# Attention scores per head on 64 rows of the array with plain keys, and the adaLN sums of layer 1 beside the dense SwiGLU

## The chip, the core and the metric

The kernel runs on one core of a Trainium2 chip. The metric is the device time of one execution in microseconds, from the first to the last instruction and what lies around them; the tensors start and end in the chip's main memory.

## The reference, cut to what matters

Two decoder layers over 256 tokens of width 1024, in fp32. Each layer takes six modulation vectors (shift, scale and gate, for the mixer and for the feed-forward part) from one product of a 1024-vector with a 1024 x 6144 matrix. Layer 0 ends in a dense SwiGLU, layer 1 in a mixture of eight experts.

```python
c_act = jax.nn.silu(c)
for l in range(DEPTH):                                    # 2 layers
    mod = (c_act @ w_ada[l] + b_ada[l])[:, None, :]
    sh_a, sc_a, g_a, sh_f, sc_f, g_f = jnp.split(mod, 6, axis=-1)
    h = rmsnorm(x, norm_mix[l]) * (1.0 + sc_a) + sh_a
    x = x + g_a * hybrid_mixer(h, ...)
    h = rmsnorm(x, norm_ffn[l]) * (1.0 + sc_f) + sh_f
    f = swiglu(h, ...) if l % 2 == 0 else moe_swiglu(h, ...)
    x = x + g_f * f

# one of the four mixers (4 heads of 64); the others differ in mask, bias or weighting
sco = jnp.einsum('bqhd,bshd->bhqs', qb, k) * scale
p = masked_softmax(sco, s_idx[None, :] <= t[:, None])
o = jnp.einsum('bhqs,bshd->bqhd', p, v)
```

Per layer five score products of this kind are made: stick-breaking (`c`), dilated (`b`), forgetting (`d`), and the selected and window branches of sparse attention (`s`, `w`, whose keys and values all heads share).

## The kernel before, in words

Features lie on partitions, 8 tiles of 128 x 256 tokens. A weight comes in 1 MB pieces into a buffer (`raw`), and ScalarE and VectorE split each half of it into a rounded fp32r part and its remainder (tiles `w`); every projection is then three fp32r matmuls of 256 columns (`mm3`: high x high, high x low, low x high). A ring of four such half pieces lets the split run up to three halves ahead of TensorE. The expert stage works on raw fp32 weights instead.

The program is a row of such chunks: 12 input chunks (`pcq`, `pck`, `pt`), 16 merge gates (`mg`) with four branch projections (`br`) between them, four output chunks (`wo`), then for layer 0 eleven rounds of `w1`, `w3` and `w2` (tiles `fa`, `fg`, `f`), then layer 1 in the same way, then the experts. Beside it run generators ("threads"): one for each attention unit, and `ada_thread` for the modulation vectors that are not needed at once. `Weave` puts their steps between the chunks: it keeps a clock of its own for each engine (`Clock`, with a cost for each instruction) and takes a step when its inputs are ready by that clock. This settles each engine's order of instructions when the program is built; on the chip every engine goes through its own list in order. At some places a chunk cannot go on without a thread, and `until` then takes the thread's steps at once, ready or not: before each branch projection, and before the last `wo` and the last `w2` chunk, where all threads must have ended.

One modulation vector is one sum of `ada_thread`: four 1 MB loads into the one buffer `aux` (the next load starts when VectorE has read the last one), eight VectorE instructions that add a row of 1024 weights times a scalar into `adaacc`, then four matmuls with ones (`ada`), a copy, two transposes (`adat`) and an addition (`mod`). `ADA_MIX` and `ADA_FFN` list the sums (layer, vector) for the two mixers and for the dense SwiGLU, and `STEP_MIX` and `STEP_FFN` the least distance of two loads by the clock of `Weave`. `GAPS` lists vectors made in another way, on TensorE, at the norms (`adag`).

Scores: `transp_k` writes the keys of two heads into a zero-padded block (`kT`, 128 rows x 2 x 256), so that one matmul over all 128 rows yields both heads' scores side by side: queries 0 to 127 against 128 keys (bank `s0`), queries 128 to 255 against 256 keys (banks `s1a`, `s1b`). `softmax` or `stick` makes the weights, `pT` transposes them (`tc`, `tb`, `td`, `ts`, `tw`), and `pv` multiplies them with the values: two heads stand on the two column halves of the array (64 columns each), in matmuls of 128 columns (`oc`, `ob`, `od`, `oa`). All of these are plain fp32, where one matmul is two instructions of TensorE.

Of the kernel before, what the change touches and what calls it, by code (L numbers as in the profile page):

```python
# [21 lines left out]
F32 = mybir.dt.float32  # L22
# [28 lines left out]

ADA_MIX = (((0, 2), (0, 4), (0, 3)), ((1, 4), (1, 3)))
ADA_FFN = ((1, 1), (1, 0))
STEP_MIX = (14.0, 18.0)
STEP_FFN = 15.0
GAPS = ((0, 5), (1, 2), (1, 5))
# [232 lines left out]
class Clock:  # L289
# [216 lines left out]
def trunk(ctx, tc, A):  # L506
# [462 lines left out]
    def mixer(l, mb, mp, pre):  # L969
# [83 lines left out]

        def key_blocks(t, ps):

            for j in range(2):
                r = slice(j * DH, (j + 1) * DH)
                sc.activation(t[r, :, j, :], ps[r, :].rearrange("p (a k) -> p a k", a=2), AF.Copy)
# [23 lines left out]


        def scores(name, q, k, kshared=None):
            tk = [None]
            yield lambda: rx.take(3, tk, name)
            s0 = px(name + "s0")
            s1 = [px(name + "s1a"), px(name + "s1b")]
            for p in range(2):
                kt = k[:, p if kshared is None else kshared]  # L1090
                pe.matmul(s0[:, p * S:(p + 1) * S], q[:, p, 0:P], kt[:, :, 0:P], start=True, stop=True)
            yield
            for p in range(2):
                kt = k[:, p if kshared is None else kshared]
                pe.matmul(s1[p], q[:, p, P:S], kt, start=True, stop=True)
                yield
            cm["S" + name] = (s0, s1, tk)

        def softmax(name, m0, m1, gate=None, out=None):
# [23 lines left out]
            for a in range(2):  # L1123
                pp = p1[:, 2 * a:2 * a + 2, :]
# [4 lines left out]
                dv.tensor_reduce(mx[:, 4 + 2 * a:6 + 2 * a], pp, axis=AX.X, op=OP.max, negate=True)  # L1129
                yield  # L1130
                exps(1, p1, (2 * a, 2 * a + 1))
                yield
# [12 lines left out]
        def stick(name):  # L1145
# [12 lines left out]
            gp.memset(u1[:, :, S:S + 1], 1.0)  # L1158
            sc.activation(t0, s0.rearrange("p (h k) -> p h k", h=NH), AF.Tanh, scale=0.0625)
            yield  # L1160
            for a in range(2):
                sc.activation(t1[:, 2 * a:2 * a + 2, :], s1[a].rearrange("p (h k) -> p h k", h=2), AF.Tanh, scale=0.0625)
                yield
# [43 lines left out]
        def pv(mi, name, parts, extra=None):  # L1207

            ko_ = [None]
            yield lambda: rO.take(1, ko_, name)  # L1210
            yield "sync"
            ps = pt("o" + name)
            n_mm = 0
            for p in range(2):
                for i in range(2):
                    for j in range(2):
                        h = 2 * p + j
                        out = ps[j * DH:(j + 1) * DH, p * S + i * P:p * S + (i + 1) * P]
                        ops = []
                        for (t0, t1, _), v in parts:  # L1220
                            ops.append((v(0, h), t0[:, h, i * P:(i + 1) * P]))
                            if i:
                                ops.append((v(1, h), t1[:, h, :]))
                        if extra is not None:
                            ops.append(extra(h, i))
                        for n, (lh, rh) in enumerate(ops):
                            pe.matmul(out, lh, rh, start=(n == 0), stop=(n == len(ops) - 1), tile_position=(0, j * DH))
                        n_mm += len(ops)
# [119 lines left out]

        def cmp_extra(h, i):
            return (cm["vc"][:, h, :], cm["pcT"][:, i * P:(i + 1) * P])  # L1350

# [37 lines left out]

        def caus0():  # L1390
            return C("C")[:, None, :].to_broadcast([P, NH, P])

# [17 lines left out]
        def unit_b():  # L1410
# [10 lines left out]
            rq1.give(tk)  # L1421
            yield from softmax("b", C("ln0")[:, None, :].to_broadcast([P, NH, P]),
                               lambda a: C("ln1")[:, None, :].to_broadcast([P, 2, S]))
# [4 lines left out]
        def unit_d():  # L1428
# [12 lines left out]
            FB, kp = cm["FB"]  # L1441
            yield from softmax("d", FB[:, :, 0:P], lambda a: FB[:, 2 * a:2 * a + 2, P:384], out=(FB, kp))
            yield from pT("d")
# [11 lines left out]
        def unit_a():  # L1455
# [12 lines left out]
            yield from scores("s", TP["ar"], TP["kk"], 0)  # L1468
            yield from softmax("s", caus0(), caus1, g3[:, :, :, 1])
# [4 lines left out]
            yield from softmax("w", caus0(), caus1, g3[:, :, :, 2])  # L1474
            yield from pT("w")
# [36 lines left out]
        else:  # L1512
            ps = pm("pck")
            feat_chunk(("in", l, 1), ps)
        key_blocks(ckT, ps)
        mark("ck")
# [676 lines left out]
```

## Time and profile before

| | before |
|---|---|
| timed, median of 3 | 1500.13 us (1496.19 to 1501.11) |
| profiled execution, own time | 1492.01 us |
| its span, first to last instruction | 1490.2 us |
| TensorE matmul busy | 1428.5 us (96%) |
| VectorE busy | 654.9 us (44%) |
| ScalarE busy | 501.9 us (34%) |
| DMA | 446.67 MB, mean 300 GB/s |

A busy share is an average over stages: start (to 37 us of the span), mixer of layer 0 (to about 291), dense SwiGLU (to about 491), mixer of layer 1 (to about 756), experts (to the end). TensorE is busy nearly all the time in the first four, while the DMA engines are nearly full only among the experts.

### The profile page before, as it was taken

The page shows a single profiled execution, that of the slowest core. Times are in us where ns is not written, and L with a number is a line of the kernel's source. Part 1 is how long each engine was busy: PE and PEld are TensorE (multiplying, and loading weights), DVE is VectorE, ACT ScalarE, POOL GpSimd, SP SyncE. Part 2 cuts the span into 40 slices and gives each one's busy share as a digit, 9 for nine tenths or more (in the row PEclk, how much of TensorE's full clock was granted, in tenths as well). Part 3 has the DMA queues.
Part 4 walks back from the last instruction along what each step waited for, and adds up shares of the span by engine and source line. Part 5 has one row for each costly group of instructions (what it writes and reads, how often), then busy time and mean ns, then how long its engine had stood idle before and what let it go on. Part 6 is the DMA issues. An engine that isn't in the chain of part 4 may idle for free. (4 is left out here: it accounts for less than half of the span.)

```text
span 1490.2 us, 28386 instructions
## 1 busy us (share of the span) xinstructions
PE 1428.5 (96%) x12156; PEld 1078.0 (72%) x12156; DVE 654.9 (44%) x1167; ACT 501.9 (34%) x996; POOL 56.2 (4%) x58
## 2 busy tenths in 40 slices
PE   7999999999999999999989999989999999999996
PEld 6998998899999899998975555445555555555553
DVE  5797787666665698677641111111111111111111
ACT  3645553354444554655431121111111111111110
POOL 0000011200000100011200000000000000000000
PEclk9999999999999999999999999999999999999998
DMA  9574747787671465554987999999999998989940
GB/s 385 217 264 145 251 173 268 310 305 274 234 247 61 174 222 218 172 197 142 356 333 318 419 419 419 419 419 420 420 416 379 414 420 348 394 344 420 420 200 33
DMA packets 73778, 446.67 MB, mean 300 GB/s; under 512 B 8080, under 2 KB 8464, under 8 KB 29072
## 3 DMA queue, kind: packets, MB, share of 16 engines
q1 hardware_dynamic: 72896, 443.76, 76.1%
q8 instruction: 122, 2.00, 0.5%
q10 hardware_dynamic: 720, 0.59, 0.1%
q14 instruction: 40, 0.33, 0.1%
HBM read 443.27 MB, written 1.05 MB: 298 GB/s over the span
## 5 line engine op out<-in xcount | busy, mean ns | idle before, releaser
L393 PE MATMUL uv<-raw,x 128*64 128x256 f32 x2816 | 340.3, 383 | 8.7 <-DMA raw<-in_moe_w 4.5
L393 DVE TENSOR_TENSOR w<-raw,w 128x1024 fp32r<-128x1024 f32 (+1 forms) x210 | 258.0, 1242 | 105.9 <-ACT w L393 105.5
L393 PEld LDWEIGHTS uv<-raw,x 128*64 128x64 f32 x2816 | 200.9, 137 | 136.8 <-issue 48.6
L393 ACT ACTIVATE w<-raw 128x1024 fp32r<-128x1024 f32 (+1 forms) x210 | 217.4, 1047 | 105.8 <-PE fa L393 16.6
L393 DVE TENSOR_TENSOR es<-es,uv 128x128 f32<-128x128 f32 x88 | 25.4, 288 | 436.2 <-ACT es L393 436.2
L393 PE MATMUL mg<-hh,w 128*128 128x256 f32 x1024 | 188.9, 283 | 4.9 <-DVE w L393 4.2
L393 PE MATMUL y<-raw,at 128*64 128x512 f32 x704 | 169.8, 601 | 11.8 <-PEq L1952 8.1
L393 PEld LDWEIGHTS mg<-hh,w 128*128 128x128 f32 x1024 | 158.6, 189 | 7.9 <-DVE w L393 5.0
L393 PE MATMUL mg<-hl,w 128*128 128x256 f32 x512 | 142.9, 279 | 0.0
L393 ACT ACTIVATE at<-at 128x128 f32<-128x128 f32 x88 | 24.4, 278 | 301.0 <-PE at L393 301.0
L393 PE MATMUL pt<-w,hh 128*128 128x256 f32 (+1 forms) x640 | 113.7, 280 | 0.0
L393 PEld LDWEIGHTS y<-raw,at 128*64 128x64 f32 x704 | 47.4, 136 | 81.1 <-issue 70.8
L393 PEld LDWEIGHTS pt<-w,hh 128*128 128x128 f32 x640 | 97.7, 188 | 1.4 <-issue 1.4
L393 PEld LDWEIGHTS mg<-hl,w 128*128 128x128 f32 x512 | 96.6, 189 | 1.0 <-issue 1.0
L393 PE MATMUL pt<-w,hl 128*128 128x256 f32 (+1 forms) x320 | 89.2, 279 | 0.0
L393 ACT ACTIVATE es<-uv 128x128 f32<-128x128 f32 x88 | 24.4, 278 | 139.6 <-PE uv L393 139.6
L393 PE MATMUL uvo<-raw,x 128*32 128x256 f32 x1056 | 65.9, 380 | 0.0
L393 PE MATMUL fa<-hh,w 128*128 128x256 f32 x352 | 65.7, 285 | 0.0
L393 PE MATMUL fg<-hh,w 128*128 128x256 f32 x352 | 64.0, 281 | 0.0
L393 PE MATMUL f<-fah,w 128*128 128x256 f32 x352 | 63.9, 281 | 0.0
L393 DVE SCALAR_TENSOR_TENSOR adaacc<-aux,cact,adaacc 128x1024 f32<-128x1024 f32 x49 | 63.5, 1297 | 0.0
L393 PEld LDWEIGHTS pt<-w,hl 128*128 128x128 f32 x320 | 60.2, 188 | 0.0
(403 smaller groups left out, 2060.3 us busy)
## 6 DMA issues: line engine op xcount, KB each, us to landing
raw<-in_moe_w SPq DMA_DIRECT2D x263, 1024.0 KB, 16.7
raw<-in_w_in SPq DMA_DIRECT2D x54, 1024.0 KB, 5.0
aux<-in_w_ada SPq DMA_DIRECT2D x48, 1024.0 KB, 7.2
raw<-in_ffn_w SPq DMA_DIRECT2D x33, 1024.0 KB, 5.2
raw<-in_w_branch SPq DMA_DIRECT2D x8, 1024.0 KB, 5.1
raw<-in_w_out SPq DMA_DIRECT2D x8, 1024.0 KB, 5.1
raw<-in_w_in_tail SPq DMA_DIRECT2D x2, 576.0 KB, 3.8
xT<-in_x SPq DMA_DIRECT2D x1, 1024.0 KB, 5.3
```

The lines of the kernel that those rows point to most:

```text
L393: r = f(*args, **kw)
```

## The change: what it does

**Scores.** Keys are kept plain (two heads on the two halves of the partitions, no zeros). Each head has a matmul of its own over 64 rows, at row 0 or row 64 of the array; heads alternate between the halves, and the two halves write to different banks (`s0a`, `s0b`; `s1a`, `s1b`, which now hold heads 0, 2 and 1, 3). `s0b` is a bank of another pool. `softmax` and `stick` read the first block in two instructions in place of one.

**Values.** `pv` takes both query blocks in one matmul where it can (256 or 512 columns) and alternates the two column halves at every matmul.

**Sums.** Layer 1's vectors 4 and 3 move from the second mixer to the dense SwiGLU, whose `ada_thread` has four sums in place of two; its step goes from 15 to 9.5. The second mixer has none. The cost of a matmul in `Clock` now counts the share of rows as well.

```diff
-ADA_MIX = (((0, 2), (0, 4), (0, 3)), ((1, 4), (1, 3)))
-ADA_FFN = ((1, 1), (1, 0))
+ADA_MIX = (((0, 2), (0, 4), (0, 3)), ())
+ADA_FFN = ((1, 1), (1, 0), (1, 4), (1, 3))
 STEP_MIX = (14.0, 18.0)
-STEP_FFN = 15.0
+STEP_FFN = 9.5
...
-            return 2.4e-3 + c * (out.partition_size() / P if tiled else 1.0)
+            return 2.4e-3 + c * (out.partition_size() * ins[0].partition_size() / (P * P) if tiled else 1.0)
...
-        kT = {n: mp.tile([P, 2, 2, S], F32, name=n) for n in ("kT0", "kT1")}
-        for t in kT.values():
-            gp.memset(t, 0.0)
-        ckT = kT["kT0"]
+        ckT = mp.tile([P, 2, S], F32, name="ckT", tag="kT0")
...
-            t = kT[tag]
-            key_blocks(t, ps)
+            t = mp.tile([P, 2, S], F32, name=name, tag=tag)
+            sc.activation(t, ps.rearrange("p (a k) -> p a k", a=2), AF.Copy)
...
-            s0 = px(name + "s0")
+            s0 = [px(name + "s0a"), pa(name + "s0b")]
             s1 = [px(name + "s1a"), px(name + "s1b")]
-            for p in range(2):
-                kt = k[:, p if kshared is None else kshared]
-                pe.matmul(s0[:, p * S:(p + 1) * S], q[:, p, 0:P], kt[:, :, 0:P], start=True, stop=True)
...
+            def prod(out, h, q0, n):
+                p, j = divmod(h, 2)
+                r = slice(j * DH, (j + 1) * DH)
+                pe.matmul(out, q[r, p, q0:q0 + P], k[r, p if kshared is None else kshared, 0:n], start=True, stop=True,
+                          tile_position=(j * DH, 0))
...
+            for h in range(NH):
+                prod(s0[h % 2][:, h // 2 * P:(h // 2 + 1) * P], h, 0, P)
+            yield
+            for h in range(NH):
+                prod(s1[h % 2][:, h // 2 * S:(h // 2 + 1) * S], h, P, S)
...
-            dv.scalar_tensor_tensor(p0, s0.rearrange("p (h k) -> p h k", h=NH), 0.125, m0, op0=OP.mult, op1=OP.add)
+            for a in range(2):
+                dv.scalar_tensor_tensor(p0[:, a::2, :], s0[a][:, 0:S].rearrange("p (h k) -> p h k", h=2), 0.125, m0(a),
+                                        op0=OP.mult, op1=OP.add)
...
+            def run(ops):
+
+                for n in range(len(ops[0])):
+                    for j in range(2):
+                        cols, q0, lh, rh = ops[j][n]
+                        out = ps[j * DH:(j + 1) * DH, :].rearrange("p (a q) -> p a q", a=2)[:, cols, q0:]
+                        pe.matmul(out, lh, rh, start=(n == 0), stop=(n == len(ops[0]) - 1), tile_position=(0, j * DH))
```

The built programs show where the instructions went. First TensorE, at the stick-breaking scores of the second mixer, between two input chunks (`pt`). Before:

```order
L393 MATMUL pt_5703<-w_5606,hl 128x256
L393 MATMUL cs_5733<-kT_5566,cqT 128x256 x2
L393 MATMUL cs1a<-kT_5566,cqT 128x512
L393 MATMUL cs1b<-kT_5566,cqT 128x512
L393 MATMUL pt_5703<-w_5635,hh 128x256 x2
```

Of the changed kernel, at the same place:

```order
L393 MATMUL pt_5746<-w_5653,hl 128x256
L393 MATMUL cs0a<-ckT,cqT 128x128
L393 MATMUL cs0b<-ckT,cqT 128x128
L393 MATMUL cs0a<-ckT,cqT 128x128
L393 MATMUL cs0b<-ckT,cqT 128x128
L393 MATMUL cs1a<-ckT,cqT 128x256
L393 MATMUL cs1b<-ckT,cqT 128x256
L393 MATMUL cs1a<-ckT,cqT 128x256
L393 MATMUL cs1b<-ckT,cqT 128x256
L393 MATMUL pt_5746<-w_5682,hh 128x256 x2
```

The place is the same; four matmuls with 1536 columns in all became eight with 1536 columns in all, each on half of the rows.

Second VectorE, at the end of the dense SwiGLU: `fact` and `fal` are the last round's product and its remainder, the two `w` behind them the second half of the last `w2` piece and the first half of the next layer's first input piece, `xT` the residual after the last `w2` chunk. Before:

```order
L393 TENSOR_TENSOR fal_5326<-fact_5324,fah_5325 128x512
L393 TENSOR_TENSOR w_5330<-raw_4910,w_5330 128x1024
L393 TENSOR_TENSOR w_5359<-raw_4973,w_5359 128x1024
L393 SCALAR_TENSOR_TENSOR xT<-f_3422,mod_3589,xT 128x256 x2
L393 SCALAR_TENSOR_TENSOR xT<-f_3423,mod_3589,xT 128x256 x2
```

Of the changed kernel (`aux_5237`, `aux_5389` and so on are loads that follow each other in the one buffer `aux`):

```order
L393 TENSOR_TENSOR w_5331<-raw_4904,w_5331 128x1024
L393 SCALAR_TENSOR_TENSOR adaacc_5206<-aux_5237,cact,adaacc_5206 128x1024
L393 TENSOR_TENSOR w_5361<-raw_4967,w_5361 128x1024
L393 SCALAR_TENSOR_TENSOR adaacc_5206<-aux_5237,cact,adaacc_5206 128x1024
L393 SCALAR_TENSOR_TENSOR adaacc_5206<-aux_5389,cact,adaacc_5206 128x1024 x2
L393 SCALAR_TENSOR_TENSOR adaacc_5206<-aux_5393,cact,adaacc_5206 128x1024 x2
L393 COPY adaacc_5206<-ada_5399 128x256
L393 TENSOR_TENSOR mod_5408<-adat_5405,bada 128x8
L393 TENSOR_SCALAR adaacc_5410<-aux_5397,cact 128x1024
L393 SCALAR_TENSOR_TENSOR adaacc_5410<-aux_5397,cact,adaacc_5410 128x1024
L393 SCALAR_TENSOR_TENSOR adaacc_5410<-aux_5413,cact,adaacc_5410 128x1024 x2
L393 SCALAR_TENSOR_TENSOR adaacc_5410<-aux_5417,cact,adaacc_5410 128x1024 x2
```

Two more instructions (on `aux_5421`), a copy and a `mod` follow, and only then `xT`. So the second half of the third sum and the whole fourth sum stand in one piece ahead of the residual, and they read six loads (`aux_5389` to `aux_5421`) one after the other.

Third TensorE at the same end of the SwiGLU, of the changed kernel (before, `f` chunk follows `f` chunk with nothing between):

```order
L393 MATMUL f_3419<-fal_5143,w_5269 128x256
L393 MATMUL f_3419<-fah_5142,w_5269 128x256
L393 MATMUL ada_5399<-adaacc_5206,cst 32x256 x4
L393 MATMUL adat_5405<-cst,adaacc_5206 128x128 x2
L393 MATMUL ada_5425<-adaacc_5410,cst 32x256 x4
L393 MATMUL adat_5431<-cst,adaacc_5410 128x128 x2
L393 MATMUL f_3416<-fah_5326,w_5298 128x256
```

Both sums' matmuls and transposes now stand between the last but one and the last `w2` chunk.

## Rows read from the trace of the kernel before

**Rows 1.** The page: the span.

```profile
span 1490.2 us, 28386 instructions
```

**Rows 2.** Busy time by stage: first mixer, dense SwiGLU, second mixer.

```profile
37.00:291.00 254.00, 246.77 (x2150) 233.27 (x2148) 198.68 (x296) 132.99 (x229) 22.02 (x16) 1.00 0.65 234
291.00:495.00 204.00, 203.09 (x1759) 197.84 (x1759) 127.47 (x150) 91.33 (x107) 3.72 (x5) 0.98 0.60 216
495.00:756.00 261.00, 254.75 (x2215) 241.09 (x2214) 193.92 (x311) 138.40 (x239) 25.14 (x25) 0.99 0.60 219
```

**Rows 3.** TensorE's waits, second mixer (total us, times, longest).

```profile
PE mg L393 <- DVE w L393: 2.9, 2, 2.4
...
PE ch L393 <- DMA aux<-in_nsa_ck_w: 1.0, 1, 1.0
```

**Rows 4.** Timeline of TensorE, stick-breaking scores of layer 1 (start, length).

```profile
514.71 0.28 PE L393 MATMUL pt<-w,hl 128*128 128x256 f32 x1
...
516.54 1.02 PE L393 MATMUL cs1b<-kT,cqT 128*128 128x512 f32 x2
...
517.63 0.28 PE L393 MATMUL pt<-w,hl 128*128 128x256 f32 x1
```

**Rows 5.** Timeline of TensorE, stick-breaking values of layer 1.

```profile
577.48 0.28 PE L393 MATMUL mg<-hh,w 128*128 128x256 f32 x1
...
577.68 1.58 PE L393 MATMUL oc<-Tc,vt 128*64 128x128 f32 x24
...
579.42 0.28 PE L393 MATMUL mg<-hl,w 128*128 128x256 f32 x1
```

**Rows 6.** Timeline of TensorE, sparse attention's values of layer 1.

```profile
715.74 0.28 PE L393 MATMUL mg<-hh,w 128*128 128x256 f32 x1
...
720.85 0.28 PE L393 MATMUL mg<-hl,w 128*128 128x256 f32 x1
```

**Rows 7.** The chain that ended last: an expert's matmuls on column halves.

```profile
1420.45 1.73 PE uv L393 x16
```

**Rows 8.** The tile `aux` in the dense SwiGLU: duration ns min/median/max, first, last start.

```profile
L393 DVE SCALAR_TENSOR_TENSOR adaacc<-aux,cact,adaacc x14: 1273/1279/1281, 332.7 to 447.7; 128x1024 f32<-128x1024 f32 x14
...
L393 DVE TENSOR_SCALAR adaacc<-aux,cact x2: 747/748/749, 329.8 to 398.2; 128x1024 f32<-128x1024 f32 x2
```

**Rows 9.** The same view: landing of its loads; then DMA issues, 447 to 490 us.

```profile
DMA to landing us min/median/max: 5.2/7.0/11.9
...
raw<-in_w_in SPq DMA_DIRECT2D x3, 1024.0 KB, 4.7
```

**Rows 10.** Timeline of VectorE and of SyncE's queue around 348 us.

```profile
347.49 1.28 DVE L393 SCALAR_TENSOR_TENSOR adaacc<-aux,cact,adaacc 128x1024 f32<-128x1024 f32 x1
...
348.80 0.38 SPq L393 DMA_DIRECT2D aux<-in_w_ada  x1
```

**Rows 11.** Timeline of VectorE, end of the SwiGLU.

```profile
481.48 1.23 DVE L393 TENSOR_TENSOR w<-raw,w 128x1024 fp32r<-128x1024 f32 x1 [0.26 <-ACT w L393]
483.11 1.23 DVE L393 TENSOR_TENSOR w<-raw,w 128x1024 fp32r<-128x1024 f32 x1 [0.41 <-ACT w L393]
```

**Rows 12.** Timeline of TensorE: first and last of the final 96 `f` matmuls.

```profile
478.94 0.28 PE L393 MATMUL f<-fah,w 128*128 128x256 f32 x1
...
490.13 0.28 PE L393 MATMUL f<-fah,w 128*128 128x256 f32 x1
```

**Rows 13.** Timeline, how a sum ends: second mixer's last.

```profile
661.70 0.64 PE L393 MATMUL ada<-adaacc,cst 128*32 128x256 f32 x8
...
662.49 0.42 DVE L393 COPY adaacc<-ada 128x256 f32<-128x256 f32 x1
...
664.66 0.44 PE L393 MATMUL adat<-cst,adaacc 128*128 128x128 f32 x2
```

**Rows 14.** Busy time by 2 us: TensorE after its gap at a norm.

```profile
300.00:302.00 2.00, 2.00 (x14) 1.37 (x7) 1.81 (x5) 1.89 (x5) 0.74 (x1) 0.50 1.02 418
...
304.00:306.00 2.00, 2.00 (x20) 2.00 (x19) 1.38 (x4) 2.00 (x4) 0.62 (x1) 1.00 1.01 406
```

More of the change, by code (lines that the diff above doesn't have):

```diff
@@ L1052, in transp @@
             mark(name)
[L1054 to L1058, printed above, removed]
         def transp_k(name, srcs, tag, flip):
@@ L1086, in scores @@
             yield lambda: rx.take(3, tk, name)
-            s0 = px(name + "s0")
+            s0 = [px(name + "s0a"), pa(name + "s0b")]
             s1 = [px(name + "s1a"), px(name + "s1b")]
-            for p in range(2):
-                kt = k[:, p if kshared is None else kshared]
-                pe.matmul(s0[:, p * S:(p + 1) * S], q[:, p, 0:P], kt[:, :, 0:P], start=True, stop=True)
+            def prod(out, h, q0, n):
[5 more added lines that the diff above has]
+                prod(s0[h % 2][:, h // 2 * P:(h // 2 + 1) * P], h, 0, P)
             yield
[L1093 to L1096, printed above, removed]
+            for h in range(NH):
+                prod(s1[h % 2][:, h // 2 * S:(h // 2 + 1) * S], h, P, S)
+            yield
             cm["S" + name] = (s0, s1, tk)
@@ L1128, in softmax @@
                     rx.give(tk)
-                dv.tensor_reduce(mx[:, 4 + 2 * a:6 + 2 * a], pp, axis=AX.X, op=OP.max, negate=True)
+                dv.tensor_reduce(mx[:, 4 + a:8:2], pp, axis=AX.X, op=OP.max, negate=True)
                 yield
-                exps(1, p1, (2 * a, 2 * a + 1))
+                exps(1, p1, (a, a + 2))
                 yield
@@ L1158, in stick @@
             gp.memset(u1[:, :, S:S + 1], 1.0)
-            sc.activation(t0, s0.rearrange("p (h k) -> p h k", h=NH), AF.Tanh, scale=0.0625)
+            for a in range(2):
+                sc.activation(t0[:, a::2, :], s0[a][:, 0:S].rearrange("p (h k) -> p h k", h=2), AF.Tanh, scale=0.0625)
             yield
             for a in range(2):
-                sc.activation(t1[:, 2 * a:2 * a + 2, :], s1[a].rearrange("p (h k) -> p h k", h=2), AF.Tanh, scale=0.0625)
+                sc.activation(t1[:, a::2, :], s1[a].rearrange("p (h k) -> p h k", h=2), AF.Tanh, scale=0.0625)
                 yield
@@ L1212, in pv @@
             ps = pt("o" + name)
-            n_mm = 0
-            for p in range(2):
-                for i in range(2):
+            def run(ops):
[4 more added lines that the diff above has]
+                        pe.matmul(out, lh, rh, start=(n == 0), stop=(n == len(ops[0]) - 1), tile_position=(0, j * DH))
+            if extra is not None:
+                ops = ([], [])
+                for j in range(2):
+                    for (t0, t1, _), v in parts:
+                        ops[j].append((slice(0, 2), 0, v(0, 0), t0[:, j::2, :]))
+                        ops[j].append((slice(0, 2), P, v(1, 0), t1[:, j::2, :]))
+                    for p in range(2):
+                        ops[j].append((slice(p, p + 1), 0, *extra(2 * p + j)))
+                run(ops)
+            else:
+                for p in range(2):
+                    ops = ([], [])
                     for j in range(2):
                         h = 2 * p + j
-                        out = ps[j * DH:(j + 1) * DH, p * S + i * P:p * S + (i + 1) * P]
-                        ops = []
                         for (t0, t1, _), v in parts:
[L1221 to L1228, printed above, removed]
+                            ops[j].append((slice(p, p + 1), 0, v(0, h), t0[:, h:h + 1, :]))
+                            ops[j].append((slice(p, p + 1), P, v(1, h), t1[:, h:h + 1, :]))
+                    run(ops)
             for (_, _, kt), _ in parts:
@@ L1347, in cmp_attn, with cmp_extra @@
             yield
-        def cmp_extra(h, i):
-            return (cm["vc"][:, h, :], cm["pcT"][:, i * P:(i + 1) * P])
+        def cmp_extra(h):
+            return (cm["vc"][:, h, :], cm["pcT"][:, None, :])
         def fox():
@@ L1388, in fox, with caus0 @@
             cm["FB"] = (FB, kp)
-        def caus0():
-            return C("C")[:, None, :].to_broadcast([P, NH, P])
+        def caus0(a):
+            return C("C")[:, None, :].to_broadcast([P, 2, P])
         def caus1(a):
@@ L1421, in unit_b @@
             rq1.give(tk)
-            yield from softmax("b", C("ln0")[:, None, :].to_broadcast([P, NH, P]),
+            yield from softmax("b", lambda a: C("ln0")[:, None, :].to_broadcast([P, 2, P]),
                                lambda a: C("ln1")[:, None, :].to_broadcast([P, 2, S]))
@@ L1441, in unit_d @@
             FB, kp = cm["FB"]
-            yield from softmax("d", FB[:, :, 0:P], lambda a: FB[:, 2 * a:2 * a + 2, P:384], out=(FB, kp))
+            yield from softmax("d", lambda a: FB[:, a::2, 0:P], lambda a: FB[:, a::2, P:384], out=(FB, kp))
             yield from pT("d")
@@ L1468, in unit_a @@
             yield from scores("s", TP["ar"], TP["kk"], 0)
-            yield from softmax("s", caus0(), caus1, g3[:, :, :, 1])
+            yield from softmax("s", caus0, caus1, g3[:, :, :, 1])
             yield "sync"
@@ L1473, in unit_a @@
             yield from pT("s")
-            yield from softmax("w", caus0(), caus1, g3[:, :, :, 2])
+            yield from softmax("w", caus0, caus1, g3[:, :, :, 2])
             yield from pT("w")
@@ L1514, in mixer @@
             feat_chunk(("in", l, 1), ps)
-        key_blocks(ckT, ps)
+        sc.activation(ckT, ps.rearrange("p (a k) -> p a k", a=2), AF.Copy)
         mark("ck")
```

2 lines of the change are left out of this document (1 added, 1 removed).

## The prediction

> **What bounds the kernel now.** I read the busy time by stage first. In the two mixers and the dense SwiGLU, TensorE's matmuls are busy 246.8 of 254, 203.1 of 204 and 254.8 of 261 us, while VectorE, the next engine, has 198.7, 127.5 and 193.9 us [rows 2]. So in these stages time is what TensorE's list takes, plus a few microseconds in which it waits. The waits were read next: in the second mixer it waits 2.9 us for VectorE's weight splits and 1.0 us for a load of compression weights that queues behind the sums' loads; no other wait there is above 1.0 [rows 3]. The reader should see two things. Work taken off TensorE in a mixer shortens the run by nearly that much, since what follows (the expert stage and its loads) starts that much earlier. And anything that makes TensorE stand still in the SwiGLU is paid in full, because it stands still there for less than 1 us now.
>
> **The change part by part.** *Scores.* From the last matmul before the stick-breaking scores to the third one behind them pass 517.63 - 514.71 = 2.92 us [rows 4]. Three ordinary steps take 0.35 of that: the final 96 `f` matmuls of the SwiGLU are (490.13 - 478.94) / 95 = 0.118 us apart [rows 12]. The scores cost 2.57 us, 1536 columns at 1.67 ns. After the change the same 1536 columns run as eight matmuls on two halves of the rows. If the halves run side by side this is 1.28 us, if not 2.57. The trace has no pair on row halves. The nearest row is a pair on column halves in the expert stage: 16 instructions of 256 columns in 1.73 us, 0.108 each [rows 7], where one alone on the array would take 0.213 (half of 256 columns at 1.67 ns); column halves run side by side in full. I take the same for row halves.
>
> What a change of the array's form costs is seen at the values: the stick-breaking ones, 24 instructions of 128 columns on column halves, take 579.42 - 577.48 - 2 x 0.118 = 1.70 us [rows 5], and would take 1.28 side by side in full. The 0.42 above it is entering, leaving and an imperfect alternation; I charge 0.4 for each score product. So 2.57 becomes 1.68, and ten of them (five per layer) give back 8.9 us. At the ends: 12.9 if there is no such charge, and a loss of 4 if the halves take turns and the charge is paid. The Trainium skill, TensorEngine Tiling (Array Packing), section Theoretical Speedup and section Key Properties, has up to 2x for a contraction of 64 rows but says that changing the tiling mode drains TensorE; the excess of 0.42 us in rows 5 agrees with a drain and bounds it. By the first sentence alone the gain would be 12.9, with the drain it is what I take.
>
> *Values.* The sparse unit's take 720.85 - 715.74 - 2 x 0.118 = 4.87 us [rows 6]; its 4096 columns side by side are 3.41. With a strict alternation and 0.4 for the change of form it should be 3.8, which is 1.1 less, twice: 2.1 us. The other three units per layer stand at 1.70 already and I give them nothing (at most 0.4 each). The smaller edits (one key copy for two, no clearing of the key blocks, one more VectorE instruction per softmax) lie on engines with slack in [rows 2] and are costed at nothing; if VectorE were the bound, the extra instruction would be some 0.1 us, eight times.
>
> *Sums out of the second mixer.* There TensorE loses two sums' own matmuls and transposes, 0.64 + 0.44 us each [rows 13], 2.2 in all. VectorE loses 2 x (0.75 + 7 x 1.28) = 19.4 us [rows 8] and SyncE's queue eight loads of 1 MB, so the two waits of [rows 3] should mostly go; I take 3.0 with smaller ones, bounds 0 and 6 (the idle part of 261 us in [rows 2]).
>
> *Sums into the dense SwiGLU.* This is where I see the result. Two sums there run today from 329.8 to 447.7 us, some 118 us for eight loads [rows 8], nearly 15 us for each, although a load lands in 7.0 us (median) and is read in 2.6. The loads wait their turn in SyncE's list behind weight pieces whose buffers are not free, so a smaller step does not bring them faster; and by the order listed above the third sum starts only near the end. Then all threads must end before the last `w2` chunk. TensorE's list has both sums' matmuls there, and VectorE's has a chain that nothing overlaps: six loads into one buffer, each issued when VectorE has read the one before.
>
> The chain by the clock of the trace before: VectorE ends the last `w2` split at 481.48 + 1.23 = 482.7 [rows 11], adds one row of `aux_5237` (1.28), splits one input half (1.23), adds the second row (1.28): 486.5. From there six loads. A load lands after 5.2 us at best in this stage, 7.0 in the median, beside weight loads; weight loads in the quiet end of the stage take 4.7 [rows 9]. In the chain nothing else is in the queue, so I take 5.2. A read is 2 x 1.28, once 0.75 + 1.28 [rows 8]. From VectorE's end to the next issue is 348.80 - (347.49 + 1.28) = 0.03 us [rows 10]; with the way back I take 0.1. The sum is 6 x 5.2 + 5 x 2.56 + 2.03 + 6 x 0.1 = 46.6, to 533.1. Then a sum's end: 0.79 from its matmuls to the copy, 0.42 for the copy [rows 13], some 0.6 for the transposes and the first matmul: 534.9. TensorE reaches this point when 48 of the 96 `f` matmuls are done, at 478.94 + 48 x 0.118 = 484.6 [rows 12]. It stands still for **50.3 us**.
>
> The Trainium skill, DMA: Bandwidth & Descriptors, section Anatomy of one DMA, has about 2.0 us of fixed cost plus the bytes at 436 GB/s for a transfer on another path; for 1 MB this is 4.4 us as an estimate, and the trace's 4.7 and 5.2 lie above it. By it the six loads would be 4.8 us shorter, and the run still slower.
>
> After such a stop the clock is low. At the norm before the SwiGLU the granted clock was 0.50 (1.2 GHz) at 300 to 302 us and 1.00 (2.4 GHz) at 304 to 306 [rows 14], with TensorE partly idle ahead of it. Four microseconds at half speed in the last `w2` chunk cost 2.0 us.
>
> *The sum.* 50.3 + 2.0 - 8.9 - 2.1 - 2.2 - 3.0 = **+36.1 us**. The profiled execution took 1492.0 us by its own time (span 1490.2 [rows 1]), which gives 1528.1; it ran 8 us under the median of the timed runs, so against 1500.1 it is **1536 us**.
>
> **The rivals.** *The row halves take turns.* For it: no row shows two row halves at once. Against it: the column halves do run at once. The scores then cost 2.57 + 0.4 each, 13 us more than I take, and the run is at 1549.
>
> *The chain is shorter than it looks.* If a lone load lands in 4.7 us, the clock costs nothing, the changes of form are free and the second mixer's waits go whole, the terms move by 3.0 + 2.0 + 4 + 3: 12 less, 1524. For it: the 4.7 of the weight loads; against it: no load of `aux` was under 5.2.
>
> *The second sequence of loads is slowed.* If each lands in the median of 7.0 us, the chain is 10.8 longer: 1547. Against it: that median is of loads that share the queue.
>
> *Faster than before.* The mechanism is VectorE as the second mixer's real bound: TensorE counted as busy while it trails VectorE's weight splits, so that taking 19.4 us off VectorE shortens the stage by as much. With the 8.9 + 2.1 + 2.2 above that is 33 us, and the stop of 52 still leaves +20, 1520. It decides only from a gain of 52 us on, or with the stop under 33, clock included: six loads and their reads in some 27 us, 4.5 each. The rows give 7.7 each.
>
> *The change does not do what it says*, in that no sum is late: this would be the case if the loads came at 9.5 us. The order of the built program excludes it.
>
> **How the numbers follow.** The forecast as summed holds 0.68; row halves in turns 0.11; loads at the median 0.08; the shorter chain, with or without VectorE as the bound, 0.09; faster 0.02; no change 0.02. The range goes from the shorter chain counted from the lowest timed run, 1496 + 24 = 1520, to the two dear cases with some of each other in them, 1556. A difference under 0.3% (4.5 us) is about what a measurement of this kernel cannot tell from no change; slower by more has 0.96, within it 0.02, faster by more 0.02.
>
> **What would show it.** In the profile after: a slice or two of the page in the middle with TensorE nearly idle; TensorE's longest wait before `ada` or `adat` with VectorE's `adaacc` as its releaser, and VectorE's before `adaacc` with the `aux` loads, about 5 us each, six times; `cs0a` to `cs1b` in about 1.7 us with a pitch near 0.11 for 256 columns; `oa` in 3.8; in the second mixer no wait for `ck` weights. I am wrong if the six loads land side by side with the SwiGLU's matmuls, if `adat` is not waited for, or if the mixers shrink by more than 25 us in all.

## The result, and the profile after

The changed kernel takes 1541.76 us (median of 4 runs, 1538.29 to 1544.95), the kernel before on the same chip 1499.76 us (4 runs, 1496.19 to 1501.11): a ratio of 1.0293, with a 95% interval of 1.0271 to 1.0314. It is 42 us slower; the forecast was 36 us slower, 1536 us. The profiled execution took 1544.95 us by its own time, the longest of the four.

The page of the changed kernel, its span, the busy time of the engines, and the two rows in tenths over 40 equal slices:

```profile
span 1543.1 us, 28296 instructions
...
PE 1430.5 (93%) x12108; PEld 1074.9 (70%) x12108; DVE 647.9 (42%) x1175; ACT 496.3 (32%) x990; POOL 49.9 (3%) x54
...
PE   8999997999996199999998999988999999999996
...
PEclk9999999899998599999998999999999999999997
```

TensorE is busy for about as long as before (1428.5 us there), in a span 53 us longer. The hole is in slices 13 and 14, each 38.6 us: the end of the dense SwiGLU.

Busy time by stage of the changed kernel, which answers to [rows 2] (first mixer, SwiGLU, second mixer; each ends at the same event as there, and the first begins at 37.00 in both):

```profile
37.00:294.60 257.60, 244.63 (x2139) 231.54 (x2138) 192.96 (x304) 130.85 (x226) 19.90 (x16) 0.98 0.65 234
294.60:550.90 256.30, 207.68 (x1779) 199.73 (x1779) 147.51 (x170) 91.18 (x107) 3.72 (x5) 0.89 0.57 203
550.90:804.00 253.10, 247.03 (x2171) 234.57 (x2170) 173.89 (x295) 135.51 (x236) 22.81 (x23) 0.99 0.53 192
```

The SwiGLU grew by 52.3 us and the second mixer shrank by 7.9, as foreseen to within some 3 us. The first mixer, which should have shrunk by 5.5, grew by 3.6. Of these 3.6, 1.6 belong to the start, which ended later in this execution: the `pcq` matmul at 37.16 us of the kernel before begins here at 38.77.

TensorE's waits over the whole run of the changed kernel (total us, times, longest):

```profile
PE ada L393 <- DVE adaacc L393: 47.0, 2, 29.5
...
PE tw L393 <- DVE Pw L393: 6.5, 2, 6.4
...
PE wo L393 <- DVE w L393: 3.3, 2, 3.0
```

The first wait is the stop that was forecast. The second was not: in the first mixer TensorE waits 6.4 us for VectorE's weights of the window product, and the 3.0 in the third row follow inside the output projection. The cause is the second subject of the experiments.

The stop, in the timeline of TensorE of the changed kernel (start, length, in brackets the idle time before it and what ended it):

```profile
487.70 0.28 PE L393 MATMUL f<-fah,w 128*128 128x256 f32 x1
...
505.48 1.08 PE L393 MATMUL ada<-adaacc,cst 128*32 128x256 f32 x8 [17.50 <-DVE adaacc L393]
...
537.34 1.08 PE L393 MATMUL ada<-adaacc,cst 128*32 128x256 f32 x8 [29.54 <-DVE adaacc L393]
...
539.30 0.56 PE L393 MATMUL f<-fah,w 128*128 128x256 f32 x1
```

VectorE in the same stretch:

```profile
488.18 1.28 DVE L393 SCALAR_TENSOR_TENSOR adaacc<-aux,cact,adaacc 128x1024 f32<-128x1024 f32 x1
494.82 2.61 DVE L393 SCALAR_TENSOR_TENSOR adaacc<-aux,cact,adaacc 128x1024 f32<-128x1024 f32 x2 [5.37 <-DMA aux<-in_w_ada]
502.82 2.61 DVE L393 SCALAR_TENSOR_TENSOR adaacc<-aux,cact,adaacc 128x1024 f32<-128x1024 f32 x2 [5.39 <-DMA aux<-in_w_ada]
...
534.59 2.61 DVE L393 SCALAR_TENSOR_TENSOR adaacc<-aux,cact,adaacc 128x1024 f32<-128x1024 f32 x2 [5.44 <-DMA aux<-in_w_ada]
```

Six loads of 1 MB go through one buffer: VectorE waits 5.4 us for a load, reads it in 2.6, and only then is the next one issued, 8.0 us a turn. TensorE stands from 487.70 + 0.12 to 539.30, 51.5 us.

TensorE at the stick-breaking scores of layer 1 in the changed kernel, to set against [rows 4], and at the sparse values, against [rows 6]:

```profile
570.45 0.28 PE L393 MATMUL pt<-w,hl 128*128 128x256 f32 x1
570.65 0.37 PE L393 MATMUL cs0a<-ckT,cqT 64*128 64x128 f32 x1
570.66 0.37 PE L393 MATMUL cs0b<-ckT,cqT 64*128 64x128 f32 x1
...
572.50 0.28 PE L393 MATMUL pt<-w,hl 128*128 128x256 f32 x1
...
742.31 0.28 PE L393 MATMUL mg<-hh,w 128*128 128x256 f32 x1
...
746.33 0.28 PE L393 MATMUL mg<-hl,w 128*128 128x256 f32 x1
```

The two row halves start 0.01 us apart. By the same reckoning as in the prediction a score product takes 572.50 - 570.45 - 0.35 = 1.70 us (2.57 before) and the sparse values 746.33 - 742.31 - 0.24 = 3.78 us (4.87 before).

### The profile page after: what moved, and what is told of

Read it like the earlier page. It is cut to its first block, busy times and chain, and to the rows that moved or that the text cites. A ratio compares the mean times of both kernels' runs of the same rounds, so it can differ in the third digit from the quotient of the medians.

```text
span 1543.1 us, 28296 instructions
## 1 busy us (share of the span) xinstructions
PE 1430.5 (93%) x12108; PEld 1074.9 (70%) x12108; DVE 647.9 (42%) x1175; ACT 496.3 (32%) x990; POOL 49.9 (3%) x54
## 5 line engine op out<-in xcount | busy, mean ns | idle before, releaser
L393 PEld LDWEIGHTS y<-raw,at 128*64 128x64 f32 x704 | 46.9, 136 | 81.7 <-issue 69.7
```

The lines of the kernel that those rows point to most:

```text
L393: r = f(*args, **kw)
```

## The experiments

Each time stands beside runs of the kernel before on the same chip; the ratio is to those.

**Which part costs.** `e1_scores_only` is the changed kernel with the old tables of sums, `e2_sums_only` the kernel before with the new tables.

```diff
-ADA_MIX = (((0, 2), (0, 4), (0, 3)), ())
-ADA_FFN = ((1, 1), (1, 0), (1, 4), (1, 3))
-STEP_FFN = 9.5
+ADA_MIX = (((0, 2), (0, 4), (0, 3)), ((1, 4), (1, 3)))
+ADA_FFN = ((1, 1), (1, 0))
+STEP_FFN = 15.0
```

> The changed kernel with the tables of sums and the step of the kernel before: scores on row halves and the new values stay, two sums stand in the SwiGLU and two beside the second mixer again. My theory (the sums cost all of it, the scores give back): TensorE's wait for the sums' last chain, 47.0 us in the changed kernel, is gone, and the run is at 1500 - 8.9 - 2.1 = 1489 us. The changed kernel's first mixer, which ends 3.6 us later where I expected 5.5 earlier, should come back here too, since the order there is the same; with it the run is at some 1497. Rival: the row halves take turns, so that scores cost 13 us more than I take: 1502 or above, and the score units each 2.6 us or more from first to last instruction.

> The kernel before with only the new tables of sums and the step of 9.5: scores and values as before. My theory: all four sums of layer 1 stand in the SwiGLU, the last two run in one chain of some six loads before the last chunk of second weights, TensorE waits some 47 us there for VectorE's accumulator, and the second mixer is 5 us shorter: 1500 + 52 - 5 = 1547 us. Rival: most of the loss comes from scores and values or from the planner's order that they bring, and this one is near 1500.

Measured: 1497.69 us for `e1_scores_only` (ratio 1.0011, 0.9996 to 1.0026), 1544.78 us for `e2_sums_only` (1.0333, 1.0306 to 1.0359). TensorE's longest wait in `e2_sums_only`, by its list of waits:

```profile
PE ada L393 <- DVE adaacc L393: 46.0, 2, 28.8
```

So the sums alone cost 48 us (1547 us expected) and make up the whole loss. Scores and values neither cost nor gain anything as a whole: the 1489 us of the plain theory was wrong, the 1497 that counts the first mixer's loss was right as a number. But in the trace of `e1_scores_only` the second mixer gives too little as well: from the end of the SwiGLU to the router pass 271.5 us, 273.8 before, a gain of 2.3 where 5.5 were forecast. No run here looks into that.

**What the stop is made of.** `e9_three_sums` puts one of the four sums back beside the second mixer, so that two loads are left for the end where six were. `e4_second_buffer` keeps all four and gives their loads a second buffer during the SwiGLU, taken from the weights.

```diff
 # e9_three_sums
-ADA_MIX = (((0, 2), (0, 4), (0, 3)), ())
-ADA_FFN = ((1, 1), (1, 0), (1, 4), (1, 3))
+ADA_MIX = (((0, 2), (0, 4), (0, 3)), ((1, 3),))
+ADA_FFN = ((1, 1), (1, 0), (1, 4))
 # e4_second_buffer
-    NSLOT, NWH, NWX, NX = 3, 4, (0, 0), (4, 4)
+    NSLOT, NWH, NWX, NX = 3, 4, (0, 0), (3, 4)
+                st.lane("aux")[1].append((fp, "fx0"))
                 ffn(fp, n2, g2)
+                st.lane("aux")[1].remove((fp, "fx0"))
```

> The changed kernel with three sums in the SwiGLU and one, (1, 3), beside the second mixer. By the order of loads, two of the third sum's loads are left for the chain before the last chunk of second weights, where six were. My theory (the stop is a chain of loads and reads in turn, 8.0 us each): TensorE's wait is the first of the two of the changed kernel, 17.5 us, the second (29.5 us) is gone, and the run is at 1508 to 1515 us. Rival (the stop has a fixed part, such as the change of work at the stage's end, and is not made of loads): the stop stays above 30 us and the run above 1525.

> The changed kernel with a second buffer for the sums' loads during the SwiGLU (one of its four extra weight buffers is given to them). The order of instructions before the last chunk stays, so that the last two sums are still one chain of about six loads. My theory (a chain of load and read in turn through one buffer, 8.0 us each in the changed kernel, of which 5.4 is the load and 2.6 the read): with two buffers the read lies beside the next load, the chain goes at the load's pace of about 5.2 and starts one load earlier, so that the stop falls from 52 to 27 to 33 us and the run to 1518 to 1524. Rival (the transfers are short of bandwidth, or the queue's hand-over sets the pace): a load takes 8 us with two in flight, the stop stays at 45 to 52 us and the run at 1537 to 1545.

Measured: 1516.03 us (ratio 1.0129, 1.0108 to 1.0150), 1 us above what was expected, and 1519.38 us (1.0162, 1.0136 to 1.0187), as expected. TensorE's wait with three sums:

```profile
PE ada L393 <- DVE adaacc L393: 17.1, 1, 17.1
```

and with the second buffer:

```profile
PE ada L393 <- DVE adaacc L393: 21.6, 2, 13.6
```

VectorE with the second buffer, three of the last five reads of the chain:

```profile
494.90 2.61 DVE L393 SCALAR_TENSOR_TENSOR adaacc<-aux,cact,adaacc 128x1024 f32<-128x1024 f32 x2 [2.56 <-DMA aux<-in_w_ada]
...
507.38 2.60 DVE L393 SCALAR_TENSOR_TENSOR adaacc<-aux,cact,adaacc 128x1024 f32<-128x1024 f32 x2 [1.84 <-DMA aux<-in_w_ada]
...
510.68 2.61 DVE L393 SCALAR_TENSOR_TENSOR adaacc<-aux,cact,adaacc 128x1024 f32<-128x1024 f32 x2 [0.70 <-DMA aux<-in_w_ada]
```

Four loads fewer take 47.0 - 17.1 = 29.9 us off the wait: the stop is loads and reads in turn. With two buffers, four turns (two more reads begin between these rows, at 500.00 and 502.94) take 510.68 - 494.90 = 15.8 us, 3.9 us each in place of 8.0.

**The stop is not needed.** `e3_late_sums_run_on` is the changed kernel with one condition: before the last `w2` chunk the program asks for the one sum that the next norm needs, not for all.

```diff
             if last:
-                wv.until(lambda: not wv.threads)
+                wv.until(lambda: (1, 0) in mod)
```

> The changed kernel with one condition changed: before the last chunk of second weights the program waits only until the sum (1, 0), which the next norm needs, is there, and not until every thread has ended; the last two sums run on beside the second mixer. My theory: the stop of 52 us is gone, the two sums cost the second mixer about 5 us as they did in the kernel before, and the run is at 1489 to 1498 us, that of the run with the old tables. Rival: the loads are what is short, and the same wait comes back at the end of the second mixer or before its output projection: above 1520, with a wait of tens of us of TensorE for VectorE's accumulator elsewhere.

Measured: 1490.57 us (ratio 0.9960, 0.9942 to 0.9978). The stop is gone and does not come back: TensorE's longest wait for VectorE's `adaacc` is 1.4 us. From the end of the SwiGLU to the router pass 266.4 us, as in the changed kernel (266.0), though two sums run there, to 612.6 us: beside the first half of this mixer they make it no longer. It is the first version faster than the kernel before.

**Do row halves need an alternating list?** `e5_halves_not_in_turn` is `e1_scores_only` with the heads in the order 0, 2, 1, 3.

```diff
-            for h in range(NH):
+            for h in (0, 2, 1, 3):
                 prod(s0[h % 2][:, h // 2 * P:(h // 2 + 1) * P], h, 0, P)
...
-            for h in range(NH):
+            for h in (0, 2, 1, 3):
                 prod(s1[h % 2][:, h // 2 * S:(h // 2 + 1) * S], h, P, S)
```

> The kernel of the run with the old tables of sums, with the heads of each score product in the order 0, 2, 1, 3: two products on the upper row half come first, then two on the lower, where they stood in turn before. Same matmuls, same banks. My theory (the row halves run side by side because neighbours in TensorE's list lie on different halves): a score product costs half way between 1.70 and 2.57 + 0.4 us, some 0.6 to 1.3 us more each, ten times, of which the first mixer hides what it waits for anyway: 1500 to 1511 us against 1497.7. Rival (the order does not matter, because TensorE holds a queue for each half): the same 1.70 us for each product, 1497 to 1499.

Measured: 1498.26 us (ratio 1.0010, 0.9994 to 1.0027): my theory fell. Its timeline of TensorE, where the list has all of `cs0a` ahead of `cs0b`:

```profile
520.01 0.28 PE L393 MATMUL pt<-w,hl 128*128 128x256 f32 x1
520.21 0.37 PE L393 MATMUL cs0a<-ckT,cqT 64*128 64x128 f32 x1
520.23 0.37 PE L393 MATMUL cs0b<-ckT,cqT 64*128 64x128 f32 x1
520.43 0.27 PE L393 MATMUL cs0a<-ckT,cqT 64*128 64x128 f32 x1
520.44 0.27 PE L393 MATMUL cs0b<-ckT,cqT 64*128 64x128 f32 x1
...
522.16 0.28 PE L393 MATMUL pt<-w,hl 128*128 128x256 f32 x1
```

The recorded starts alternate all the same, and the product takes 522.16 - 520.01 - 0.35 = 1.80 us, 0.1 more than in turn.

**Why the first mixer gives nothing back.** TensorE's busy time from 105.0 to 265.5 us (about from the last input chunk to the output projection, in both kernels), of the kernel before:

```profile
105.00:265.50 160.50, 154.75 (x1368) 144.75 (x1367) 124.60 (x176) 84.84 (x166) 16.52 (x13) 1.00 0.62 216
```

and of the changed kernel:

```profile
105.00:265.50 160.50, 150.73 (x1339) 140.52 (x1339) 118.91 (x189) 82.83 (x162) 14.39 (x13) 0.98 0.62 216
```

TensorE has 4.0 us less to do there, and waits 4.0 us more. VectorE in the changed kernel, before the window product's transposes (`tw`) begin at 251.97:

```profile
234.74 0.42 DVE L393 SCALAR_TENSOR_TENSOR Pw<-ws0a,cstm 128x256 f32<-128x256 f32 x1
...
236.12 4.62 DVE L393 TENSOR_TENSOR w<-raw,w 128x1024 fp32r<-128x1024 f32 x4
240.66 1.28 DVE L393 SCALAR_TENSOR_TENSOR adaacc<-aux,cact,adaacc 128x1024 f32<-128x1024 f32 x1
243.33 1.23 DVE L393 TENSOR_TENSOR w<-raw,w 128x1024 fp32r<-128x1024 f32 x1 [1.39 <-ACT w L393]
244.47 1.28 DVE L393 SCALAR_TENSOR_TENSOR adaacc<-aux,cact,adaacc 128x1024 f32<-128x1024 f32 x1
245.67 1.22 DVE L393 TENSOR_TENSOR w<-raw,w 128x1024 fp32r<-128x1024 f32 x1
246.80 0.68 DVE L393 SCALAR_TENSOR_TENSOR Pw<-ws1a,cstm 128x512 f32<-128x512 f32 x1
...
251.13 1.90 DVE L393 TENSOR_TENSOR Pw<-Pw,su 128x512 f32<-128x512 f32 x3
```

The softmax begins at 234.7 and ends at 253.0, because its second half stands behind six weight splits and two rows of a sum. In the kernel before, the whole softmax stands ahead of the last splits:

```profile
239.88 1.18 DVE L393 TENSOR_TENSOR Pw<-Pw,su 128x512 f32<-128x512 f32 x1
240.99 5.72 DVE L393 TENSOR_TENSOR w<-raw,w 128x1024 fp32r<-128x1024 f32 x4
```

TensorE's two waits in the changed kernel, at the window product's transposes and inside the output projection, which begins at 265.98:

```profile
251.97 0.44 PE L393 MATMUL tw<-cst,Pw 128*128 128x128 f32 x1 [6.35 <-DVE Pw L393]
...
272.34 0.73 PE L393 MATMUL wo<-mh,w 128*128 128x256 f32 x2 [3.03 <-DVE w L393]
```

Two causes fit: VectorE has too much to do there, or the list has it in a bad order. Six runs went into this.

`e6_old_cost_formula` and `e7_run_on_old_formula` are `e1_scores_only` and `e3_late_sums_run_on` with the old cost formula, which leads the planner to other orders.

```diff
-            return 2.4e-3 + c * (out.partition_size() * ins[0].partition_size() / (P * P) if tiled else 1.0)
+            return 2.4e-3 + c * (out.partition_size() / P if tiled else 1.0)
```

> The kernel of the run with the old tables of sums, with the planner's old formula for the cost of a matmul on part of the array (it prices a score product on row halves at twice its time, and so sets other orders; no instruction is other). Theory: the first mixer of the changed kernel gives nothing back because the softmax of the window product is late at the mixer's end (TensorE waits 6.4 us for VectorE's Pw and then 3.0 for a weight split); that comes from where the planner puts the window product, behind the 24 branch matmuls, and here it stands some 200 matmuls ahead of its transposes. The wait of 6.4 us is gone and the run is at 1490 to 1494 us. Rival (VectorE has too much to do at that place whatever the order): the wait comes back under another name, and the run stays at 1496 to 1499.

> The run in which the late sums run on beside the second mixer, with the planner's old formula too: a candidate that could beat both kernels. Theory: what the old formula gives back in the first mixer (some 6 us) adds to the 6 us that this run already gains: 1483 to 1487 us. Rival (the second mixer's order, which the formula changes as well, loses what the first gains): 1489 to 1493.

Measured: 1495.77 us (ratio 0.9977, 0.9959 to 0.9994) and 1495.14 us (0.9984, 0.9970 to 0.9998). Both expected times failed: the first lies between theory and rival, the second above both. The wait for `Pw` is gone in both, but in its place TensorE waits in the first mixer of `e6_old_cost_formula` 3.1 us before `mg` for weight splits and 2.2 before `br` for VectorE's `brt`, and the stretch from the last input chunk to the output projection takes 162.7 us instead of 160.2. So the old formula moves the wait and does not bring the gain back. That a wait comes back under another name is what the rival of `e6_old_cost_formula` said; these two runs do not tell the causes apart.

`e10_less_vector_after` and `e11_less_vector_before` leave out three of the four loads of the sum (0, 3), in `e3_late_sums_run_on` and in the kernel before.

```diff
-        keys = deque(k for l, s in ls for k in seg(l, s))
+        loads = lambda l, s: seg(l, s)[:1 if (l, s) == (0, 3) else 4]
+        keys = deque(k for l, s in ls for k in loads(l, s))
...
-            for j in range(4):
-                key = ("ada", l, s, j)
+            for j, key in enumerate(loads(l, s)):
```

> The run in which the late sums run on, with three of the four loads of the first mixer's sum (0, 3) left out, with what VectorE would read of them (6 instructions of 1.28 us); the shift of the first dense norm is then made of a quarter of its products, and the output is not the reference's. Question: why the first mixer gives back nothing of the 5.5 us of scores and values. Theory (VectorE is behind at the end of that mixer, so that any work taken off it there shortens TensorE's wait for Pw): the wait of 6.4 us falls to 2 or less, the stretch from 105 to the output projection goes from 160 us to some 155, and the run from 1490.6 to 1483 to 1486 us. Rival (the window product's softmax is put late by the order of the program, and VectorE's total does not matter): the wait stays at 5 to 6.5 us and the run at 1489 to 1491.

> The kernel before with the same three loads of the sum (0, 3) and their reads left out (output not the reference's either): what they cost where no wait for Pw stands. Theory: VectorE is not what the first mixer of the kernel before waits for, so that it gains at most the smaller waits, 0 to 2 us: 1496 to 1500. Rival (VectorE's total bounds both kernels' first mixers): 5 us or more, 1493 or below.

Measured: 1502.84 us (ratio 1.0036, 1.0017 to 1.0055) and 1516.8 us (1.0141, 1.0103 to 1.0180). These totals say nothing on the question: other values reach the router, and the expert stage is longer (from the first to the last `uv` 702.3 and 704.9 us, 679.4 and 679.6 with all loads). The first mixers can be compared. The waits of `e10_less_vector_after` there:

```profile
PE tw L393 <- DVE Pw L393: 0.4, 1, 0.4
```

From the last input chunk to the output projection it takes 154.8 us (160.0 with all loads), the kernel before 157.0 (160.1). So less work for VectorE goes with the wait gone; but in this program the first part of the softmax's second half also stands ahead of the splits, and three loads are off the queue. For the kernel before at most 2 us were expected, and that failed: over the whole first mixer, from the first `pt` matmul to the last of the output projection, it takes 243.4 us instead of 248.5. So the work of this sum, or its loads, cost 5 us there too, where nothing waits for `Pw`.

`e12_sum_on_pool` keeps the loads and takes that sum off VectorE: ScalarE multiplies, GpSimd adds.

```diff
+                    if (l, s) == (0, 3):
+                        d = acc if j == 0 and k == 0 else w
+                        sc.activation(d, w, AF.Copy, scale=c)
+                        if d is w:
+                            gp.tensor_tensor(acc, acc, w, op=OP.add)
-                    if j == 0 and k == 0:
+                    elif j == 0 and k == 0:
```

> The run in which the late sums run on, with the sum (0, 3) of the first mixer moved off VectorE: ScalarE multiplies each row block by its column and GpSimd adds it to the accumulator; all four loads stay and the output is the reference's. It tells VectorE's work apart from the loads that the run without three of them left out as well, and could be the fastest version. Theory (VectorE's work is what makes the window product's softmax late): the wait of 6.4 us of TensorE for Pw falls to 3 or less, the output projection begins near 261 us instead of 265.8, and the run is at 1483 to 1488 us. Rival 1 (the loads were what counted): the wait stays at 5 us or more, the run at 1490. Rival 2 (GpSimd, whose additions of 512 elements take 1.5 us, needs some 3 us for each of seven, so that the sum is late for the norm): a new wait of TensorE for the accumulator or for merged, and the run at 1490 to 1496.

Measured: 1497.20 us (ratio 1.0000, 0.9982 to 1.0017), and the wait for `Pw` is 6.5 us, as with the sum on VectorE. VectorE there:

```profile
243.00 2.59 DVE L393 TENSOR_TENSOR w<-raw,w 128x1024 fp32r<-128x1024 f32 x1 [0.84 <-ACT w L393]
245.97 2.91 DVE L393 TENSOR_TENSOR w<-raw,w 128x1024 fp32r<-128x1024 f32 x1 [0.38 <-ACT w L393]
```

and GpSimd:

```profile
242.10 5.70 POOL L393 TENSOR_TENSOR adaacc<-adaacc,aux 128x1024 f32<-128x1024 f32 x2 [6.59 <-ACT aux L393]
```

Beside GpSimd's additions a split takes 2.6 to 2.9 us instead of 1.2, and what VectorE was spared is lost again. This run does not tell the two causes apart.

`e13_run_on_more_slack` is `e3_late_sums_run_on` with more slack in the planner; VectorE has the same work, in another order.

```diff
-    SLACK, AHEAD = 2.0, 0.8
+    SLACK, AHEAD = 4.0, 0.8
```

> The run in which the late sums run on, with the planner's slack for VectorE and ScalarE (how far it lets them fall behind TensorE before it holds a unit's next step back) at 4.0 instead of 2.0. In the program that it sets, the first mixer's window product stands earlier against its transposes (between them 204 full-array matmuls instead of 120), and VectorE's list has both halves of its softmax ahead of the six weight splits that stood between them before. Theory (the wait of 6.4 us comes from where those splits stand in VectorE's list, not from how much VectorE does): the wait for Pw is below 1 us, the output projection begins at 259 to 261 us instead of 265.8 and the run takes 1483 to 1487 us. Rival (VectorE has as much to do and is late for something else): the wait comes back before a branch or mixing chunk as a wait for a weight split, and the run is at 1489 to 1495 us.

Measured: 1485.75 us (ratio 0.9896, 0.9879 to 0.9913), as expected (the 204 matmuls there are a miscount; it is 216). There is no wait for `Pw` in its list, the output projection begins at 260.4, and its stretch takes 155.8 us. VectorE now:

```profile
223.12 0.68 DVE L393 SCALAR_TENSOR_TENSOR Pw<-ws1b,cstm 128x512 f32<-128x512 f32 x1
...
237.79 0.71 DVE L393 TENSOR_TENSOR Pw<-Pw,su 128x512 f32<-128x512 f32 x1
...
239.21 4.90 DVE L393 TENSOR_TENSOR w<-raw,w 128x1024 fp32r<-128x1024 f32 x3
```

The softmax ends at 238.5, ahead of the last splits and 2.7 us before `tw` begins at 241.16. From the first `pt` matmul to the last of the output projection the first mixer takes 243.0 us, where the kernel before takes 248.5 and the changed kernel 250.4: a gain of 5.5 us, which is what was forecast for this mixer. Same work, other order (in the lists of all engines, that of TensorE too): the order was enough. This is the fastest version, 1.0% below the kernel before.

## Why the prediction was right, and where it was off

**The stop.** Right in place, mechanism and size: 51.5 us against 50.3. From the end of one read to the start of the next pass 5.3 to 5.6 us, where I had 5.3 (5.2 and 0.1 for the way back); over the six loads that is 0.8 of the 1.2 us between the two, and the reads, 2.61 us and not 2.56, are most of the rest. The two runs with fewer loads and with two buffers show that it is this chain, `e3_late_sums_run_on` that the condition at the last chunk makes it a stop.

**The clock after it.** The granted clock by 2 us in the changed kernel:

```profile
539.80:542.00 2.20, 2.20 (x12) 2.20 (x11) 0.05 (x1) 0.00 (x0) 0.00 (x0) 0.50 0.00 0
542.00:544.00 2.00, 2.00 (x19) 2.00 (x19) 1.25 (x3) 0.64 (x1) 0.00 (x0) 0.98 0.00 0
```

From 539.3 to 542 TensorE ran at 0.50 (1.2 GHz); half of 2.7 us is 1.3, where I took 2.0.

**Scores and values.** 1.70 against 1.68, and 3.78 against 3.8: the row halves run side by side, and the 0.4 read from the values for a change of the array's form holds for them too (1.70 - 1.28 = 0.42). The rival in which the halves take turns is out.

**The second mixer.** TensorE's busy time fell from 254.75 [rows 2] to 247.03 us, by 7.7; the terms (half of 8.9 and of 2.1, and 2.2) make 7.7. The waits were mis-sized: I gave them 3.0, but the idle time of the stage went from 6.3 [rows 2] to 6.1 us only. The wait for the compression weights is gone, that for weight splits is 1.9 (2.9 in [rows 3]), and others came.

**The first mixer: the step that failed.** I let scores and values give back the same 5.5 us in both mixers and costed the rest at nothing, because VectorE has slack over the stage. A mean of a stage does not say that: at the end of the first mixer the planner's new order put six weight splits and two rows of a sum between the two halves of the last softmax, and TensorE waits there 6.4 us, then 3.0 inside the output projection. `e13_run_on_more_slack` shows that the order is enough to explain it, since another one with the same work brings the gain back: 4.3 us in the stretch from the last input chunk to the output projection (160.1 to 155.8), where four score products and the sparse values should give 4.6, and 5.5 over the whole mixer. That less work for VectorE would do as well is what `e10_less_vector_after` suggests, with its order and its loads changed too, and `e11_less_vector_before` shows that the slack was not free in the kernel before either.

**The sum.** With 1.2 more for the stop, 0.7 less for the clock, 2.8 for the waits and 7.5 for the first mixer (from -5.5 to 2.0, the 3.6 less the 1.6 by which the start ended later), 36.1 becomes 46.9, against 42 between the medians. The two profiles differ by 53 us, 11 more than the medians, because of where these two executions lie among their own runs (before 8 us under the median, after 3 above). About 5 of these 11 are after the router, where the programs are alike (726.3 and 731.1 us to the end of the span), and 1.6 in the start, where the granted clock was 0.50 (1.2 GHz) from 24 to 26 us in this execution of the changed kernel, and 1.00 (2.4 GHz) in the kernel before and in `e9_three_sums`, where TensorE has the same instructions up to there. The other 4 or 5 must lie in the terms as these two executions had them; where was not settled. So the total missed by 6 us where the terms missed by 11, and that smaller miss is luck.

## What to carry to other kernels

Work that is said to run "beside" a stage needs its deadline looked at: when a program waits for all side work at a stage's end, whatever is late there becomes a chain, and if it goes through one buffer each turn costs the transfer and the read. Ask there only for what the next step needs. And read slack where the critical engine will wait, in the order of the other engine's list, not as a mean over the stage: here one constant of the planner, with the same work, decided over 5 us.

## What the runs showed of the hardware

In `e5_halves_not_in_turn` TensorE starts the first matmul of the lower row half 0.02 us after the first of the upper, although one more of the upper half stands between them in the list that the program writes. The Trainium skill, PSUM — Partial Sum Buffer, section Engine vs sequencer instructions, says that matmuls start and complete in program order; the recorded starts of matmuls on different row halves here do not. Whether TensorE or its record changes the order was not settled.

A weight split of VectorE (two inputs and one output of 1024 columns) takes 1.22 us alone and 2.59 and 2.91 us beside GpSimd's additions of the same size, of which two take 5.70 us. The Trainium skill, SBUF — State Buffer, section SBUF: two separate sides, has a port pair that the two engines hold in turn for a whole instruction; these numbers agree with it. Alone such an addition takes 2.4 us; if the first split waits for the addition that began at 242.10, it ends at 242.10 + 2.4 + 1.2 = 245.7, and it ended at 245.6.

A load of 1 MB that is issued when the one before has been read keeps VectorE waiting 5.3 to 5.6 us in the changed kernel and 5.1 to 5.3 in `e9_three_sums`. With a second buffer in `e4_second_buffer` one is read every 3.9 us.
